# A WKV recurrence on one core: separate pools for k, v and outputs become one set of 19 buffers, and the order of loads and stores changes with it

## The chip, the cores and the metric

The kernel runs on one core of a Trainium2 chip. The metric is the device time of one execution, in microseconds. Four compute engines take part: PE (TensorE, matrix products), DVE (VectorE), ACT (ScalarE) and POOL (GpSimd). SP (SyncE) issues nearly all transfers. Each engine runs its own instructions in order and meets the others only through semaphores.

## The reference

For each of 16 sequences and 256 channels the reference walks along 2048 time steps. It keeps a numerator `aa`, a denominator `bb` and a running maximum `pp`, and puts out a weighted mean of the values so far:

```python
def reference(w, u, k, v):                 # k, v: (16, 2048, 256) float32
    ...
    for t in range(seq_len):
        kk, vv = k[b, t, :], v[b, t, :]
        ww = u + kk
        qq = np.maximum(pp, ww)
        e1, e2 = np.exp(pp - qq), np.exp(ww - qq)
        output[b, t, :] = (e1 * aa + e2 * vv) / (e1 * bb + e2 + 1e-08)
        ww = pp - w + kk
        qq = np.maximum(ww, kk)
        e1, e2 = np.exp(ww - qq), np.exp(kk - qq)
        aa, bb, pp = e1 * aa + e2 * vv, e1 * bb + e2, qq
```

## The kernel before

The kernel doesn't walk along time. It cuts time into 16 stretches `c` of 128 steps, and the 16 sequences into 4 groups of 4. One unit of work `n` (of `NP` = 64) is one stretch of one group: `c, p = divmod(n, 4)`. A unit's k is a tile of 128 partitions (the time steps) by 4 sequences by 256 channels, 512 KB in float32; its v and its output have the same shape and size.

Within a unit, sums along time are matrix products. On PE, `logs(n)` (L191, with the constant rows of L185) adds decay to k. On ACT, `exps(n)` (L204) takes the exponentials into a ring of 12 units, `EZR`. On DVE, `times_v(n)` (L214) multiplies them with v. Then `den` (L341) and `num` (L358) sum denominators and numerators on PE by triangular matrices. The division is done by logarithms: on ACT, `den_log` (L346) writes the logarithm of the denominator into a tile `rd`, and `den_exp` (L349) turns it in place into the reciprocal. On DVE, `mult` (L362), once for each half, multiplies the numerator in, again in place, and `store` (L365) sends the tile out. The state that goes from one stretch to the next is worked out for four units at once by small operations on POOL, DVE and ACT (`state_...`, `copy_sums`, `turn`, `turn_back`), and `inject` puts it into `EZR` by four small transfers, from POOL's queue, for the last stretch from SP's.

The order of the work is written out by hand. Loop turn `n` is called a slot here. Slots 0 to 9 (`LAG` = 10) only fill the ring. From slot 10 to 63, slot `n` takes the exponentials of unit `n` and divides unit `q = n - 10`, with the last products of `qp = n - 11`. A tail then divides the last eleven units. `later` holds the small work of the state by slot and place.

DVE reads k and v once each, and with that the raw tile is done with. `round_k(n + 2)` in slot `n` (L176) copies k of unit n+2 into a rounded tile; `cast_v` (L209) copies v to bf16. The casts are spread unevenly over four slots:

```python
        if n % 4 in (3, 0):
            cast_v(n)
        ...
        elif n % 4 < 2:
            cast_v(n + 1)
```

So a slot with n%4 = 0 has two of them, n%4 = 1 and 3 have one, and n%4 = 2 has none. DVE's order in a slot is: `mult` of the first half, what the state needs, `round_k`, `cast_v`, `mult` of the second half, `times_v`. ACT's order is: `exps`, `den_log`, `den_exp`, with small operations of the state between.

Raw tiles and outputs have pools of their own: `kpool` has 6 buffers, `vpool` 5, `rpool` (for `rd`) 8, 19 tiles of the same size in all. At the head of slot `n`, `load(n + AHEAD)` issues v of unit n+5 and k of unit n+6 (L64, L60), and right behind it `store(qp - 2)` sends out unit n-13. Loads and stores share SP's queue: an issue that waits for a buffer or a result holds up all behind it. At the very end, the output of the last unit goes out in four parts from SP's and ACT's queues (L533), two after each half.

Of the kernel before, what the change touches and what calls it, by code (L numbers as in the profile page):

```python
# [7 lines left out]
F32 = mybir.dt.float32  # L8
# [7 lines left out]
def kernel(  # L16
# [9 lines left out]
    K = tc.keep_in_program_order  # L26
    PE, DVE, SC, POOL, SP = nc.tensor, nc.vector, nc.scalar, nc.gpsimd, nc.sync

    B, T, Dm = k.shape
# [3 lines left out]
    D = 2 * Dm  # L33
    NP = 4 * NST
    RING = 12
    AHEAD = 6
    LAG = 10
    RS = 2.0 ** -20
    CAP = 54.0
    ON_DVE = (0, 1, NST - 1)  # L40

    consts = ctx.enter_context(tc.tile_pool(name="consts", bufs=1))
    kpool = ctx.enter_context(tc.tile_pool(name="kpool", bufs=AHEAD))
    vpool = ctx.enter_context(tc.tile_pool(name="vpool", bufs=5))
    vbpool = ctx.enter_context(tc.tile_pool(name="vbpool", bufs=4))
    rpool = ctx.enter_context(tc.tile_pool(name="rpool", bufs=8))
    small = ctx.enter_context(tc.tile_pool(name="small", bufs=2))
    tiny = ctx.enter_context(tc.tile_pool(name="tiny", bufs=1))
    ps = ctx.enter_context(tc.tile_pool(name="ps", bufs=1, space=bass.MemoryType.PSUM))
# [2 lines left out]
    kr_of, vr_of, VB = {}, {}, {}  # L52

    def rows_of(x, n):
        c, p = divmod(n, 4)
        return x[4 * p:4 * p + 4, c * TC:(c + 1) * TC, :].rearrange("n t d -> t n d")

    def load_k(n, queue=SP):
        kr_of[n] = kpool.tile([128, 4, Dm], F32, tag="kr", name="kr")
        K(queue.dma_start(out=kr_of[n], in_=rows_of(k, n)))  # L60

    def load_v(n, queue=SP):
        vr_of[n] = vpool.tile([128, 4, Dm], F32, tag="vr", name="vr")
        K(queue.dma_start(out=vr_of[n], in_=rows_of(v, n)))  # L64


    def load(n):
        if n - 1 < NP:
            load_v(n - 1)
        if n < NP:  # L70
            load_k(n)

    def matrix(name, dt):
        return consts.tile([128, 128], dt, tag=name, name=name)

    def fill(ap, value):
        K(DVE.memset(ap.bitcast(F32) if ap.dtype == F32R else ap, value))
# [27 lines left out]
    load_k(1)  # L107
    load_row(SP, 1, 2, u)
    load_v(0)
    for n in range(2, AHEAD):  # L110
        load_k(n)
        load_v(n - 1)
    K(SC.preload_act_table_set("natural_log_exp_and_others"))
# [34 lines left out]
    def out_matrices(*names):  # L148
        if "L" in names:
            for h in range(2):  # L150
                fill(Lx[HS * h:HS * h + HS, HS * (1 - h):HS * (2 - h)], 0.0)
        for name in names:
            x, f = I1 if name[0] == "I" else Lx, RS if name[-1] == "N" else 1.0
            mats[name] = matrix(name, BF16)
            K(DVE.tensor_single_scalar(mats[name], x, f, op=ALU.mult))
# [15 lines left out]
    def ez(n):  # L171
        return EZR[:, :, n % RING]

    def round_k(n):
        km = consts.tile([128, 4, Dm], F32R, tag=f"km{n % 2}", name="km") if n < 2 else KM[n - 2]
        K(DVE.tensor_copy(km, kr_of.pop(n)))  # L176
        KM[n] = km

    def logs(n):
        km = KM[n].rearrange("p (i n) d -> p i (n d)", i=2)  # L180

        def rows(q):
            for i in range(2):
                g = 32 * (2 * q + i)
                K(PE.matmul(half(n, q)[:, i, :], CO[g:g + 32, :],  # L185
                            WU[g:g + 32, :].unsqueeze(1).broadcast_to([32, 2, Dm]), start=True, stop=False,
                            tile_position=(g, 0), skip_group_check=True))

        def steps(q):
            for i in range(2):  # L190
                K(PE.matmul(half(n, q)[:, i, :], (NLE, NLZ)[q], km[:, i, :], start=False, stop=True,  # L191
                            skip_group_check=True))

        rows(0)
        rows(1)
        steps(0)
        steps(1)

    def exps(n):
        if n < TURNS:  # L200
            for q in range(2):
                K(SC.activation(ez(n)[:, q], half(n, q), ACT.Exp))  # L202
        else:
            K(SC.activation(ez(n)[:, 0:2], PS[:, 0:4, :].rearrange("p (q i) x -> p q i x", q=2), ACT.Exp))  # L204

    def cast_v(n):
        vb = vbpool.tile([128, 4, Dm], BF16, tag="vb", name="vb")
        vr = vr_of.pop(n)
        K(DVE.tensor_copy(vb, vr))  # L209
        VB[n] = vb  # L210

    def times_v(n):
        vb = VB.pop(n).rearrange("p (i n) d -> p i (n d)", i=2)
        K(DVE.tensor_mul(ez(n)[:, 2:4], ez(n)[:, 0:2], vb.unsqueeze(1).broadcast_to([128, 2, 2, D])))  # L214
# [16 lines left out]
    def sums(n):  # L231
        c, p = divmod(n, 4)
        t = MISC[:, 0:Dm]
        for o in range(2):
            x = 24 - 16 * o - 2 * p
            for j in range(4):
                q, i = divmod(j, 2)
                K(PE.matmul(t[32 * j:32 * j + 32, :], mats["OH"][:, x:x + 32],  # L238
                            ez(n)[:, 2 * q, i, Dm * o:Dm * o + Dm],
                            start=p == 0 and o == 0, stop=p == 3 and o == 1,  # L240
                            tile_position=(0, 32 * j), skip_group_check=True))
# [94 lines left out]
    RD = {}  # L336
# [5 lines left out]
                            skip_group_check=True))  # L342

    def den_log(n, bank=DENB):
        RD[n] = rpool.tile([128, 2, D], F32, tag="rd", name="rd")
        K(SC.activation(RD[n], bank, ACT.Ln, scale=RS))  # L346

    def den_exp(n, i=slice(0, 2)):
        K(SC.activation(RD[n][:, i, :], RD[n][:, i, :], ACT.Exp, scale=-1.0))  # L349
# [10 lines left out]
    def mult(n, bank, i):  # L360
        rd = RD[n]
        K(DVE.tensor_mul(rd[:, i, :], bank, rd[:, i, :]))  # L362

    def store(n):
        K(SP.dma_start(out=rows_of(out, n), in_=RD.pop(n).rearrange("p i (n d) -> p (i n) d", n=2)))  # L365

    later = {}
    for c in range(NST):
# [19 lines left out]
    def small_work(n, where):  # L388
        for f, c in later.pop((n, where), []):
            f(c)  # L390

    def idle_matmuls(n, bank):
        for _ in range(n):
            K(PE.matmul(bank, idle[:, 0:128], idle, start=True, stop=True, skip_group_check=True))
# [5 lines left out]
    K(DVE.scalar_tensor_tensor(WU, WUH, Rest, wuf, ALU.mult, ALU.add))  # L400
    logs(0)
    round_k(1)
    cast_v(0)
    for n in range(LAG):

        load(n + AHEAD)
        exps(n)
        if n % 4 == 0 and n:
            sums(n - 1)
        small_work(n, "act")  # L410
        small_work(n, "logs")
        logs(n + 1)
        if n % 4:
            sums(n - 1)
        small_work(n, "pe")
        idle_matmuls(2, NUMB)
        times_v(n)
        small_work(n, "chain")
        round_k(n + 2)
        small_work(n, "round")  # L420
        cast_v(n + 1)
        if n < 4:
            (state_start, lambda: out_matrices("L"), lambda: out_matrices("IdN", "LN"),
             lambda: out_matrices("Id"))[n]()

    def inverses(n):
        q, qp = n - LAG, n - LAG - 1
        if qp >= 0:
            num(qp, NUMB, 1)

        sums(n - 1)
        if n + 1 < NP:
            recip(q, lambda: small_work(n, "recip"))

    for n in range(LAG, NP):

        q, qp = n - LAG, n - LAG - 1
        load(n + AHEAD)

        if qp >= 2:  # L440
            store(qp - 2)
        if qp >= 0:
            num(qp, NUMB, 0)
        den(q)
        small_work(n, "nums")
        exps(n)
        small_work(n, "act")
        if qp >= 0:
            mult(qp, NUMB, 0)
        small_work(n, "mid")  # L450
        if n == LAG:

            inverses(n)
            small_work(n, "early")
        if n + 2 < NP:
            round_k(n + 2)

        if n % 4 in (3, 0):
            cast_v(n)
        if n + 1 == NP:  # L460
            times_v(n)
        elif n % 4 < 2:
            cast_v(n + 1)
        if n > LAG:
            inverses(n)
        if qp >= 0:
            mult(qp, NUMB, 1)
        small_work(n, "scan")
        if n + 1 < NP:
            times_v(n)  # L470
            small_work(n, "chain")
            logs(n + 1)
        small_work(n, "pe")
# [4 lines left out]
    q, c = NP - LAG - 1, NST - 1  # L478
# [4 lines left out]
    def outputs(n):  # L483
        for i in range(2):
            mult(n, nbank(n, i), i)
        store(n)

    den_log(q)
    den(q + 1, dbank(q + 1))
    sums(NP - 1)  # L490
    copy_sums(c)
    store(q - 2)
    store(q - 1)
    den_exp(q)
    den_log(q + 1, dbank(q + 1))
    tile_num(q, 0)
# [9 lines left out]
    state_offsets(c)  # L506
    state_weights(c)
    mult(q, nbank(q, 1), 1)
    store(q)
    state_chain(c)  # L510
    den(q + 3, dbank(q + 3))
    for i in range(2):
# [14 lines left out]
    n, p = NP - 1, (NP - 1) % 4  # L527
    for i in range(2):
        den_exp(n, slice(i, i + 1))
        mult(n, nbank(n, i), i)  # L530
        for j, eng in ((0, SP), (1, SC)):
            b = 4 * p + 2 * i + j
            K(eng.dma_start(out=out[b, c * TC:(c + 1) * TC, :], in_=RD[n][:, i, Dm * j:Dm * j + Dm]))  # L533
# [31 lines left out]
```

## Time and profile before

| | |
|---|---|
| time, median of 3 runs | 289.74 us (289.18 to 290.79) |
| the profiled execution: time / span | 289.65 us / 288.0 us |
| busy PE / DVE / ACT / POOL | 261.4 / 262.3 / 254.7 / 105.2 us |
| read from HBM / written | 67.12 MB / 33.55 MB |
| mean rate over the span | 353 GB/s |
| issue to landing, k / v / output (median) | 8.3 / 8.3 / 8.1 us |

The span runs from the first to the last event of the core in the trace. The busy time of an engine is the time in which it carried out an instruction; PE's is modelled. The DMA share is the mean over the core's 16 DMA engines and can read over 1, since packets overlap. A row of a timeline has the start, the length, the engine, the line of the kernel, the operation, what it writes and reads, and in brackets the idle time before it with what ended it. A row of the waits has the waiting engine and line, what it waited for, the total in us, the number of times and the longest.

### The profile page before, as it was taken

The numbers are of one execution on the slowest core, as the hardware profiler recorded it, in microseconds if no ns is written. First come the engines' busy times: TensorE is split into PE (matmuls) and PEld (weight loads), VectorE is DVE, ScalarE is ACT, GpSimd is POOL, SyncE is SP. The second block draws the span as 40 slices with busy tenths as digits, with TensorE's granted clock in tenths as the row PEclk, the third lists the DMA queues.
The fourth block names the chain that finished last, engine by engine and source line by source line (L and its number), as shares of the span: only waits on it lengthen the run. The fifth ranks groups of instructions, "written<-read, shape, count | busy, mean of one in ns | idle before, by whom it ended". The sixth has DMA issues, their size and how long they took to land. (4 is left out here: it accounts for less than half of the span.)

```text
span 288.0 us, 5023 instructions
## 1 busy us (share of the span) xinstructions
PE 261.4 (91%) x1694; PEld 119.4 (41%) x1694; DVE 262.3 (91%) x463; ACT 254.7 (88%) x252; POOL 105.2 (37%) x208
## 2 busy tenths in 40 slices
PE   5997897999999999999999999899998989998990
PEld 1443443544444544435444444344344444433430
DVE  4698999999999999999999999998999999988863
ACT  2675678999999999999999989999998999998891
POOL 7000523352534454543525364460434435233000
PEclk9799999999999999999999999999999999999997
DMA  6999999999999999999999999999999999994697
GB/s 214 353 348 350 349 331 349 331 361 375 381 369 381 372 379 378 381 379 381 378 376 381 369 381 375 377 376 371 373 374 380 374 377 380 373 383 160 201 339 245
DMA packets 103587, 101.54 MB, mean 353 GB/s; under 512 B 4285, under 2 KB 103561, under 8 KB 103561
## 3 DMA queue, kind: packets, MB, share of 16 engines
q1 hardware_dynamic: 101336, 100.45, 102.6%
q0 software_dynamic: 1920, 0.50, 0.8%
q8 instruction: 13, 0.21, 0.3%
q10 hardware_dynamic: 304, 0.27, 0.3%
q14 instruction: 14, 0.11, 0.1%
HBM read 67.12 MB, written 33.55 MB: 350 GB/s over the span
## 5 line engine op out<-in xcount | busy, mean ns | idle before, releaser
L204 ACT ACTIVATE EZR<-PS 128x2048 bf16<-128x2048 f32 x54 | 101.2, 1875 | 7.5 <-PE PS L191 6.5
L362 DVE TENSOR_TENSOR rd<-PS,rd 128x512 f32<-128x512 f32 x128 | 87.0, 687 | 6.1 <-ACT rd L349 4.7
L214 DVE TENSOR_TENSOR EZR<-EZR,vb 128x2048 bf16<-128x2048 bf16 x64 | 78.1, 1220 | 2.2 <-ACT EZR L202 1.5
L349 ACT ACTIVATE rd<-rd 128x1024 f32<-128x1024 f32 (+1 forms) x65 | 67.9, 1047 | 2.7 <-DVE rd L362 1.8
L346 ACT ACTIVATE rd<-PS 128x1024 f32<-128x1024 f32 x64 | 65.7, 1026 | 0.8 <-PE PS L341 0.8
L358 PE MATMUL PS<-EZR,LN 128*128 128x512 bf16 x128 | 48.7, 381 | 12.2 <-DVE rd L362 8.4
L331 POOL DMA_DIRECT2D EZR<-cb x60 | 36.5, 614 | 52.1 <-DVE cb L326 45.4
L176 DVE CAST km<-kr 128x1024 fp32r<-128x1024 f32 x64 | 44.7, 699 | 6.9 <-DMA kr<-in_k_dram 6.4
L191 PE MATMUL PS<-km,NLE 128*128 128x512 f32 x128 | 47.5, 453 | 2.3 <-DVE km L176 2.2
L358 PE MATMUL PS<-EZR,IdN 128*128 128x512 bf16 x128 | 48.4, 378 | 0.0
L209 DVE CAST vb<-vr 128x1024 bf16<-128x1024 f32 x64 | 43.4, 694 | 0.7 <-DMA vr<-in_v_dram 0.7
L191 PE MATMUL PS<-km,NLZ 128*128 128x512 f32 x128 | 40.6, 398 | 0.0
L341 PE MATMUL PS<-EZR,Id 128*128 128x512 bf16 x128 | 38.1, 379 | 0.0
L341 PE MATMUL PS<-EZR,L 128*128 128x512 bf16 x128 | 38.1, 379 | 0.0
L185 PE MATMUL PS<-WU,CO 32*128 32x512 bf16 x256 | 27.2, 388 | 3.4 <-DVE WU L400 2.2
L269 POOL TENSOR_TENSOR F<-LL,LL 128x32 f32<-128x32 f32 x13 | 6.7, 515 | 61.9 <-ACT LL L260 61.9
L191 PEld LDWEIGHTS PS<-km,NLZ 128*128 128x128 f32 x128 | 24.4, 191 | 5.8
L191 PEld LDWEIGHTS PS<-km,NLE 128*128 128x128 f32 x128 | 19.3, 190 | 17.3 <-issue 12.9
L238 PE MATMUL PS<-EZR,OH 128*32 128x256 bf16 x512 | 26.1, 278 | 0.1
L202 ACT ACTIVATE EZR<-PS 128x1024 bf16<-128x1024 f32 x20 | 19.4, 1019 | 7.6 <-PE PS L191 7.6
L358 PEld LDWEIGHTS <-IdN 128*128 128x128 bf16 x128 | 12.5, 97 | 28.7 <-issue 26.3
L282 POOL TENSOR_TENSOR Q<-P,F 128x64 f32<-128x64 f32 x13 | 15.7, 1205 | 15.0 <-DVE P L273 15.0
(71 smaller groups left out, 200.0 us busy)
## 6 DMA issues: line engine op xcount, KB each, us to landing
kr<-in_k_dram SPq DMA_DIRECT2D x64, 512.0 KB, 8.3
vr<-in_v_dram SPq DMA_DIRECT2D x64, 512.0 KB, 8.3
out_dram<-rd SPq DMA_DIRECT2D x63, 512.0 KB, 8.1
EZR<-cb POOLq DMA_DIRECT2D x60, 8.0 KB, 5.3
out_dram<-rd SPq DMA_DIRECT2D x2, 128.0 KB, 2.7
out_dram<-rd ACTq DMA_DIRECT2D x2, 128.0 KB, 2.2
EZR<-cb SPq DMA_DIRECT2D x4, 8.0 KB, 1.9
wuf<-in_w_dram ACTq DMA_DIRECT2D x1, 8.0 KB
```

The costliest lines, as they stand in the source:

```text
L176: K(DVE.tensor_copy(km, kr_of.pop(n)))
L185: K(PE.matmul(half(n, q)[:, i, :], CO[g:g + 32, :], WU[g:g + 32, :].unsqueeze(1).broadcast_to([32, 2, Dm]), start=True, stop=False, tile_p ...
L191: K(PE.matmul(half(n, q)[:, i, :], (NLE, NLZ)[q], km[:, i, :], start=False, stop=True, skip_group_check=True))
L204: K(SC.activation(ez(n)[:, 0:2], PS[:, 0:4, :].rearrange("p (q i) x -> p q i x", q=2), ACT.Exp))
L209: K(DVE.tensor_copy(vb, vr))
L214: K(DVE.tensor_mul(ez(n)[:, 2:4], ez(n)[:, 0:2], vb.unsqueeze(1).broadcast_to([128, 2, 2, D])))
L331: K(queue.dma_start(out=EZR[r:r + 1, 2 * q, r0:r0 + 4, :, :].rearrange("o p i (b x) -> o (p i b) x", b=4), in_=cb[x:x + 32, :]))
L341: K(PE.matmul(bank[:, i, :], mats[m], ez(n)[:, q, i, :], start=q == 0, stop=q == 1, skip_group_check=True))
L346: K(SC.activation(RD[n], bank, ACT.Ln, scale=RS))
L349: K(SC.activation(RD[n][:, i, :], RD[n][:, i, :], ACT.Exp, scale=-1.0))
L358: K(PE.matmul(bank, mats[m], ez(n)[:, q, i, :], start=q == 2, stop=q == 3, skip_group_check=True))
L362: K(DVE.tensor_mul(rd[:, i, :], bank, rd[:, i, :]))
```

## The change

The three pools go. `BUFS` = 19 tiles are allocated once, and a list `free` holds each unused one with the slot from which it may be taken. `take(slot)` hands out the tile with the lowest such number, the first in the list where several have it. `round_k` and `cast_v` return their raw tile with the current slot, `store` returns its tile with the slot plus `STORED` = 3. `den_log` takes its tile from the same list.

`loads(n)` now stands behind the casts of slot `n`, and no longer at the slot's head. It loads pairs (v, then k of the next unit) as long as the count is less than nine units ahead of the slot and enough tiles are free, with one kept back for `den_log` from slot 9 on. Stores come behind the loads of the slot. While loads remain, the store in slot `n` is unit n-14 at first, and from slot 24 on one unit later for every six slots; once all loads are issued, everything that is finished goes out. At the very end, both halves of the last reciprocal come ahead of the two products and their transfers.

```diff
-    AHEAD = 6
+    BUFS = 19
+    STORED = 3
...
-    kpool = ctx.enter_context(tc.tile_pool(name="kpool", bufs=AHEAD))
-    vpool = ctx.enter_context(tc.tile_pool(name="vpool", bufs=5))
...
-    rpool = ctx.enter_context(tc.tile_pool(name="rpool", bufs=8))
...
+    free = [(0, consts.tile([128, 4, Dm], F32, tag=f"buf{j}", name="buf")) for j in range(BUFS)]
+
+    def take(slot):
+        j = min(range(len(free)), key=lambda j: free[j][0])
+        assert free[j][0] <= slot
+        return free.pop(j)[1]
+
+    def load_k(n, slot=0):
+        kr_of[n] = take(slot)
+        K(SP.dma_start(out=kr_of[n], in_=rows_of(k, n)))
...
+    loaded = 5
+
+    def loads(slot):
+        nonlocal loaded
+        keep = 1 if slot + 1 >= LAG else 0
+        while loaded < NP and loaded - slot < 9 and sum(x <= slot for x, _ in free) >= 2 + keep:
+            load_v(loaded, slot)
+            loaded += 1
+            if loaded < NP:
+                load_k(loaded, slot)
...
-    def round_k(n):
+    def round_k(n, slot=0):
...
-        K(DVE.tensor_copy(km, kr_of.pop(n)))
+        kr = kr_of.pop(n)
+        K(DVE.tensor_copy(km, kr))
+        free.append((slot, kr))
...
-    def cast_v(n):
+    def cast_v(n, slot=0):
...
+        free.append((slot, vr))
...
     def den_log(n, bank=DENB):
-        RD[n] = rpool.tile([128, 2, D], F32, tag="rd", name="rd")
+        RD[n] = take(n + LAG).rearrange("p (i n) d -> p i (n d)", i=2)
         K(SC.activation(RD[n], bank, ACT.Ln, scale=RS))
...
-    def store(n):
-        K(SP.dma_start(out=rows_of(out, n), in_=RD.pop(n).rearrange("p i (n d) -> p (i n) d", n=2)))
+    def store(n, slot):
+        rd = RD.pop(n).rearrange("p i (n d) -> p (i n) d", n=2)
+        K(SP.dma_start(out=rows_of(out, n), in_=rd))
+        free.append((slot + STORED, rd))
...
-        load(n + AHEAD)
         exps(n)
...
-        round_k(n + 2)
+        round_k(n + 2, n)
         small_work(n, "round")
-        cast_v(n + 1)
+        cast_v(n + 1, n)
+        loads(n)
...
-        load(n + AHEAD)
-
-        if qp >= 2:
-            store(qp - 2)
         if qp >= 0:
             num(qp, NUMB, 0)
...
         elif n % 4 < 2:
-            cast_v(n + 1)
+            cast_v(n + 1, n)
+        loads(n)
+
+        while stored < (qp - 2 - max(0, n - 18) // 6 if loaded < NP else qp):
+            store(stored, n)
+            stored += 1
         if n > LAG:
             inverses(n)
...
     copy_sums(c)
-    store(q - 2)
-    store(q - 1)
+    for n in range(stored, q):
+        store(n, q + LAG)
...
     for i in range(2):
         den_exp(n, slice(i, i + 1))
+    for i in range(2):
         mult(n, nbank(n, i), i)
         for j, eng in ((0, SP), (1, SC)):
```

More of the change, by code (lines that the diff above doesn't have):

```diff
@@ L56, in rows_of, with load_v @@
         return x[4 * p:4 * p + 4, c * TC:(c + 1) * TC, :].rearrange("n t d -> t n d")
[L58 to L71, printed above, removed]
+    free = [(0, consts.tile([128, 4, Dm], F32, tag=f"buf{j}", name="buf")) for j in range(BUFS)]
[6 more added lines that the diff above has]
+        K(SP.dma_start(out=kr_of[n], in_=rows_of(k, n)))
+    def load_v(n, slot=0):
+        vr_of[n] = take(slot)
+        K(SP.dma_start(out=vr_of[n], in_=rows_of(v, n)))
+    loaded = 5
[7 more added lines that the diff above has]
+                load_k(loaded, slot)
     def matrix(name, dt):
@@ L109 @@
     load_v(0)
-    for n in range(2, AHEAD):
+    for n in range(2, 6):
         load_k(n)
@@ L424 @@
              lambda: out_matrices("Id"))[n]()
+    stored = 0
     def inverses(n):
@@ L455 @@
         if n + 2 < NP:
-            round_k(n + 2)
+            round_k(n + 2, n)
         if n % 4 in (3, 0):
-            cast_v(n)
+            cast_v(n, n)
         if n + 1 == NP:
@@ L485, in outputs @@
             mult(n, nbank(n, i), i)
-        store(n)
+        store(n, n + LAG)
     den_log(q)
@@ L508 @@
     mult(q, nbank(q, 1), 1)
-    store(q)
+    store(q, q + LAG)
     state_chain(c)
```

## The prediction

> **What bounds the kernel now.** I read the slices of the page first (DMA share, GB/s), then busy time by stretches, then the waits, and last the timeline of one slot, because only there the order of two engines shows.
>
> ```profile
> DMA  6999999999999999999999999999999999994697
> GB/s 214 353 348 350 349 331 349 331 361 375 381 369 381 372 379 378 381 379 381 378 376 381 369 381 375 377 376 371 373 374 380 374 377 380 373 383 160 201 339 245
> ```
>
> DMA is full from the second slice to 260 us and falls to 160 GB/s while the last outputs are computed. By stretches (us; PE, PEld, DVE, ACT, POOL; clock; DMA share; GB/s):
>
> ```profile
> 120.00:140.00 20.00, 19.58 (x131) 8.86 (x129) 19.70 (x36) 19.81 (x20) 8.90 (x18) 1.00 1.09 380
> ...
> 220.00:240.00 20.00, 18.33 (x124) 8.36 (x124) 18.76 (x30) 18.59 (x20) 8.58 (x17) 1.00 1.08 377
> ...
> 260.00:265.00 5.00, 4.91 (x30) 2.12 (x28) 4.36 (x15) 4.26 (x7) 1.68 (x5) 1.00 0.47 157
> ```
>
> At 120 us DVE and ACT have no gap; at 220 us both lose over a microsecond in 20 at the same DMA rate. Who waits (total, times, longest):
>
> ```profile
> ACT EZR L204 <- PE PS L191: 6.5, 11, 1.4
> DVE km L176 <- DMA kr<-in_k_dram: 6.4, 17, 0.9
> ```
>
> Of those 17 waits for k, 14 lie after 165 us. The starts of `exps(n)` (L204) in the timeline give the slots: slot 15 at 59.70, slot 41 at 162.93, slot 63 at 256.77. So the pitch is 103.23/26 = 3.970 us, then 93.84/22 = 4.265. The DMA queue explains the second: k20 is issued at 59.40 and k63 at 242.07, 43 slots of three transfers, 182.67/129 = 1.416 us each, 4.25 a slot. **Compute needs 3.97 a slot, DMA 4.25; the lead of the loads is used up near slot 41, and from there DMA sets the pace.** Now slot 25 on the two full engines:
>
> ```profile
> 99.36 1.89 ACT L204 ACTIVATE EZR<-PS 128x2048 bf16<-128x2048 f32 x1
> ...
> 100.26 0.68 DVE L362 TENSOR_TENSOR rd<-PS,rd 128x512 f32<-128x512 f32 x1
> ...
> 100.86 0.69 DVE L176 CAST km<-kr 128x1024 fp32r<-128x1024 f32 x1
> ...
> 101.28 1.06 ACT L346 ACTIVATE rd<-PS 128x1024 f32<-128x1024 f32 x1
> ...
> 101.46 0.69 DVE L209 CAST vb<-vr 128x1024 bf16<-128x1024 f32 x1
> ...
> 102.38 1.06 ACT L349 ACTIVATE rd<-rd 128x1024 f32<-128x1024 f32 x1
> ...
> 103.43 1.88 ACT L204 ACTIVATE EZR<-PS 128x2048 bf16<-128x2048 f32 x1
> ...
> 104.04 0.68 DVE L362 TENSOR_TENSOR rd<-PS,rd 128x512 f32<-128x512 f32 x1
> ```
>
> The reader is to see that the logarithm of the denominator (`den_log`, L346) starts at 101.28, while the casts of the same slot (L176, L209) end at 101.55 and 102.15. Today the two have nothing to do with each other.
>
> **What the Trainium skill says.** "DMA: Bandwidth & Descriptors", section "Anatomy of one DMA — SWDGE (gpsimd) path": DMA engines don't wait on semaphores, the issuing sequencer does, before dispatch. The trace agrees: SP's own waits name L64 and L365, the longest 5.1 us, with all later issues behind. "ScalarE: Activation LUTs", "What ACT_TABLE_LOAD costs": back-to-back ACTIVATEs overlap by some 93 ns. Here an `exps` of 1.88 is followed by its successor after 1.77 (103.43, then 105.20): 110 ns. "HBM Reference", "Specifications (TRN2)": a core alone can stream about 425 GB/s. This trace shows no more than 383 in any slice, so I use the measured 1.416 us.
>
> **The change, part by part.**
>
> *Order of the transfers: −6.5 us.* I wrote the rules of `take`, `loads` and the store loop out slot by slot. Ahead of v63 there were 46 stores, now 40. By the end of slot 20, 64 transfers are asked for, by the end of slot 59, 167: 103 in 39 slots, 2.64 × 1.416 = 3.74 us a slot, less than compute's 3.97. Loads start the stretch ahead (six more of them precede the first store), so k is no longer late. 22 slots × (4.265 − 3.970) = 6.5. What is late next is the work on ACT and DVE.
>
> *The shared buffers: a new wait of `den_log`, +11.3 us.* Before, its buffer came from a pool of its own, stored long ago. Now it takes the buffer with the lowest slot number, and loads have taken theirs first. Written out for slots 15 to 60, 26 of 46 get the buffer of a v cast in that same slot, 11 that of the k rounded in it, 9 one whose store is three slots old. ACT must wait until DVE has read it. Behind it in ACT's queue stand `den_exp` and the next `exps`; for these wait DVE's `mult` and `times_v`, and PE's next `logs`.
> The size: ACT could start `den_log` 1.77 after `exps` (2.04 where n%4 is 1, the state's Ln lies between). DVE's first `mult` starts L after `exps`; each further operation follows after 0.60, the last lasts 0.69; n%4 = 3 has a copy of 0.21 between; a hand-over takes 0.04 (DVE at 273.03 after ACT's end at 272.99). A buffer comes free at L + 1.89 after one cast, L + 2.49 after two. L was 0.90 and 0.61 in slots 25 and 26; it can't be under 0.15, as `den_exp` ends 0.11 into `exps`. With L = 0.15 the waits are 0.91 (5 slots with n%4 = 0, second cast), 0.31 (6, first cast), 0.04 (8, n%4 = 1), 0.52 (7, n%4 = 3), none for k: 4.55 + 1.86 + 0.32 + 3.64 = 10.4. With L = 0.6 the same 26 slots give 22.1 and k's 2.3: 24.4. Since a late ACT pulls L to its floor, I take 0.25: 10.4 + 26 × 0.10 = 13.0. Slot 18 takes the buffer of store 1. That is the tenth transfer after k19 (issued at 55.12, done with at 56.5), so issued near 69.3 and landed near 77.4 (8.1 later, the median of 63 stores); `den_log` wants it at 71.65 + 1.77 and the 1.8 that slots 15 to 17 have waited, 75.2: nothing to 3, I take 2. Off goes the air that ACT has: per four slots 4 × (1.77 + 0.96 + 0.95) + 0.30 + 0.27 + 0.27 = 15.56, 3.89 a slot against 3.97, 46 × 0.08 = 3.7. So 13.0 + 2 − 3.7 = 11.3. The ends: 10.4 − 3.7 = 6.7, and 17.3 (L = 0.3, 3 us for the store, no air: 14.3 + 3).
>
> *The end: −1.2 us.*
>
> ```profile
> 282.38 0.36 ACTq L533 DMA_DIRECT2D out_dram<-rd  x1
> 282.80 0.63 ACT L349 ACTIVATE rd<-rd 128x512 f32<-128x512 f32 x1 [1.84 <-DVE rd L362]
> 283.46 0.69 DVE L362 TENSOR_TENSOR rd<-PS,rd 128x512 f32<-128x512 f32 x1 [1.11 <-ACT rd L349]
> ```
>
> The second exponential stood behind ACT's own store issue, which waited for the first product. With both exponentials first, the second product follows the first (start 281.66) at 282.26 in place of 283.46. Its numerator is there (PE ends at 281.80).
>
> *Costing nothing.* In slots 0 to 10 the order of loads is the same and SP issues without a pause from 3 to 55 us, so nine ahead brings none earlier; cover: the full queue. Issuing behind the casts costs no more than the lead: late in the run k(n+5) is issued in slot n and due in slot n+3, 11.9 us for a landing of 8.3; k63, issued in slot 59, has 8 us, so 0 to 1 us if the queue is full. In slot 60 nine stores go out at once and five follow: 14 × 1.54 (0.524 MB at the 340 GB/s of 275 to 280 us) = 21.6 us, done some 10 us into the tail, where `inject` goes on the same SP queue (266.77, 10.0 after slot 63). Its rows are read 6.4 us later and need 4.4, so 2 us cover it: 0, at most +1.5.
>
> Sum: −6.5 + 11.3 − 1.2 = +3.6 on the profiled execution's 289.65 (span 288.0, 1.65 around it; the median of runs, 289.74, is 0.1 higher): **293.2 us**.
>
> **Rivals.** (a) *Faster*: the wait is covered, because DVE gets so far ahead that the cast ends before `den_log` could start. Then −6.5 − 1.2: 282; with half of the wait 287.6. It decides where waits less ACT's air fall under 7.7 us. For it: the 9 buffers from stores and 11 from k give ACT time to come back; against it: the floor of L, since DVE's first product itself waits for ACT. (b) *No change*: all waits at the floor: −6.5 + 6.7 − 1.2 = −1.0, 288.7. (c) *Much slower*: L stays at 0.6, each cast pushes the next: −6.5 + 24.4 − 3.7 − 1.2 = +13, 302.7. Against it: a waiting ACT lets DVE catch up. (d) The change doesn't reach what it says: with buffers short, loads lead by nine pairs only to slot 13 and by five at slot 54. But the 2.64 transfers a slot come from that count, so DMA still has room; should k be late again from slot 41, the wait counts in 26 slots only: 26 × 11.3/46 − 1.2 = +5.2, 294.9.
>
> **The numbers.** My forecast has 0.58, (c) 0.04, (d) 0.05: slower 0.67. Faster, (a): 0.22. Within 0.5%, (b) (1.4 us, about what a measurement of this kernel can tell from no change): 0.11. The range, 284.5 to 297, leaves out the fully covered wait (about 0.12) and the upper tail (0.07).
>
> **What would show it.** Right: L346 waits for DVE's L176 and L209 in the list of waits, over 10 us in all; no wait of km for k after 165 us; a pitch near 4.2 from slot 15 on, even in the stretch that ran at 3.97; DMA below full after 100 us; L349's last wait gone. Wrong: ACT at 19.8 of 20 us and a pitch of 3.97 to slot 63, or k still late.

## The result and the profile after

| | before | after |
|---|---|---|
| time, median | 289.86 us (4 runs) | 303.37 us (4 runs, 302.55 to 304.83) |
| ratio after / before | | 1.0469 [1.0418, 1.0521] |
| profiled execution: time / span | 289.65 / 288.0 us | 302.55 / 300.8 us |
| busy PE / DVE / ACT | 261.4 / 262.3 / 254.7 us | 258.7 / 264.1 / 255.1 us |
| `exps` of slot 15 / of slot 63 start at | 59.70 / 256.77 us | 59.99 / 269.31 us |
| pitch, slots 15 to 41 / 41 to 63 | 3.970 / 4.265 us | 4.469 / 4.233 us |

The change costs 13.5 us. The prediction had 3.6 us, with the right sign and a range that ended at 297 us. The engines do the same work; what grew is the time between slots, and almost only up to slot 41. On the page of the kernel after, the DMA slices (share in tenths, then GB/s) now read:

```profile
DMA  7999999999999999999999799999979999999697
GB/s 231 351 348 350 345 337 337 345 347 360 385 376 374 383 377 355 378 380 316 362 349 322 227 353 356 330 353 347 339 231 365 301 363 333 363 385 349 200 341 258
```

Before, 369 GB/s was the lowest slice between 72 and 259 us. Now the rate falls to 316 and 227 in slices of that stretch: DMA waits for compute. By stretches (us; PE, PEld, DVE, ACT, POOL; clock; DMA share; GB/s):

```profile
120.00:140.00 20.00, 17.41 (x120) 8.01 (x121) 18.51 (x31) 18.46 (x18) 6.82 (x15) 1.00 1.04 358
220.00:240.00 20.00, 18.07 (x123) 8.48 (x125) 18.80 (x31) 17.84 (x18) 8.66 (x17) 1.00 0.94 303
```

At 120 us, where DVE and ACT had no gap, ACT now loses 1.5 us in 20, DVE 1.5, PE 2.6. No engine took the place of DMA as the bound: all three now have gaps. The list of waits of the kernel after (engine and line, what it waited for; total, times, longest):

```profile
DVE buf L376 <- ACT buf L363: 13.3, 26, 0.9
...
ACT buf L360 <- issue: 5.9, 15, 0.8
ACT buf L360 <- PE PS L252: 5.8, 11, 0.9
...
ACT buf L360 <- PE PS L334: 3.7, 4, 1.1
...
ACT buf L360 <- DMA out_dram<-buf: 3.0, 1, 3.0
...
DVE km L188 <- DMA buf<-in_k_dram: 1.4, 3, 1.1
```

The wait for k is down from 6.4 us to 1.4, and the three waits left all lie before 40 us. Longer slots alone would do that too: experiment 2 has the old order of transfers and no late k behind 40 us either. `den_log` (L360) has 20.4 us of idle time before it, but nothing in the list says that it waits for DVE's casts. A line of its own view points to it. Before and after:

```profile
L346 ACTq EVENT_SEMAPHORE  x56: 17/17/38, 71.7 to 276.0; - x56
```

```profile
L360 ACTq EVENT_SEMAPHORE  x64: 17/1929/3511, 38.8 to 289.1; - x64
```

In front of a `den_log` stands a semaphore instruction (min, median, max ns): a wait of ACT's queue ahead of the operation. Before, 56 of the 64 had one, all but as many as `rpool` had buffers, so it seems to stand for the buffer, and it took 17 ns. Now all have one, with a median of 1929 ns. PE's result is the second thing waited for, and the list puts most of the idle time down to PE, or to "issue". So the order must be read in the timeline. Slot 31 (n%4 = 3), one engine beside the other:

```profile
132.62 1.87 ACT L217 ACTIVATE EZR<-PS 128x2048 bf16<-128x2048 f32 x1
132.85 0.44 DVE L318 TENSOR_TENSOR CB<-AB,G 128x128 bf16<-128x128 f32 x1
133.09 0.72 DVE L376 TENSOR_TENSOR buf<-PS,buf 128x512 f32<-128x512 f32 x1
133.78 0.29 DVE L340 CAST cb<-PS 128x128 bf16<-128x128 f32 x1
133.99 0.68 DVE L188 CAST km<-buf 128x1024 fp32r<-128x1024 f32 x1
...
134.59 0.69 DVE L222 CAST vb<-buf 128x1024 bf16<-128x1024 f32 x1
...
135.36 1.03 ACT L360 ACTIVATE buf<-PS 128x1024 f32<-128x1024 f32 x1 [0.88 <-PE PS L334]
...
137.38 1.86 ACT L217 ACTIVATE EZR<-PS 128x2048 bf16<-128x2048 f32 x1
```

`exps` ends at 134.49. `den_log` starts at 135.36, 0.08 after the cast of v (L222) ends at 135.28; the bracket names PE's L334, which has long been done. The next `exps` comes 4.76 after the last. The DVE product (L376) that opens the chain of casts starts 0.47 after `exps`: DVE is still at the state of the slot before (L318 ends at 133.29; its result goes through PE and comes back by the copy L340).

The prediction's L, the time from `exps` to that first product, is thus 0.47 here. (In slots 27, 39 and 51 it is 0.33, but then the copy L340 waits for PE, and the cast of v is done 2.64 after `exps` there and 2.66 here.) In slot 28 (n%4 = 0) it is 0.12:

```profile
120.23 1.86 ACT L217 ACTIVATE EZR<-PS 128x2048 bf16<-128x2048 f32 x1
120.35 0.69 DVE L376 TENSOR_TENSOR buf<-PS,buf 128x512 f32<-128x512 f32 x1 [0.50 <-ACT buf L363]
...
121.56 1.29 DVE L222 CAST vb<-buf 128x1024 bf16<-128x1024 f32 x2
122.33 1.03 ACT L360 ACTIVATE buf<-PS 128x1024 f32<-128x1024 f32 x1 [0.24 <-PE PS L252]
```

(The row with x2 is both casts; `den_log` takes the buffer of the first, done at 122.25.) And slot 18 stands for the output of unit 1, whose store has not landed:

```profile
74.24 1.86 ACT L217 ACTIVATE EZR<-PS 128x2048 bf16<-128x2048 f32 x1
79.09 1.02 ACT L360 ACTIVATE buf<-PS 128x1024 f32<-128x1024 f32 x1 [2.99 <-DMA out_dram<-buf]
...
81.20 1.87 ACT L217 ACTIVATE EZR<-PS 128x2048 bf16<-128x2048 f32 x1
```

Slot 18's pitch, from its `exps` to the next, is 6.96 us. Sorted by what the slot's `den_log` takes, the 48 pitches from slot 15 to 63 fall into few values:

| slot n%4 | what is taken | pitch, us | over the unwaited slot | slots |
|---|---|---|---|---|
| 0 | v, second cast of the slot | 4.85 | 0.97 | 5 |
| 0 | v, first cast | 4.24 | 0.36 | 6 |
| 1 | v | 4.44 | 0.38 | 8 |
| 1 | k | 4.05 | 0 | 3 |
| 2 | k | 4.10 | 0.23 | 3 |
| 3 | v | 4.75 (slot 15: 4.99) | 0.90 | 7 |
| 3 | k | 4.14 (slot 19: 3.85) | 0.28 | 5 |
| 2 | old store (slot 18) | 6.96 | 3.1 | 1 |

Slots without a wait have 3.88, 4.06, 3.87 and 3.85 for n%4 = 0 to 3, a mean of 3.915. Two of these rest on one slot each: 3.88 on slot 60, and 3.85 on slot 19, right behind the stall of slot 18. Over them, the surplus sums to 18.3 for the casts and 3.1 for slot 18.

### The profile page after: what moved, and what is told of

Read it like the earlier page. It is cut to its first block, busy times and chain, and to the rows that moved or that the text cites. A ratio compares the mean times of both kernels' runs of the same rounds, so it can differ in the third digit from the quotient of the medians.

```text
span 300.8 us, 4998 instructions
## 1 busy us (share of the span) xinstructions
PE 258.7 (86%) x1662; PEld 121.5 (40%) x1694; DVE 264.1 (88%) x463; ACT 255.1 (85%) x252; POOL 98.1 (33%) x208
## 4 chain that ended last, share of the span: by engine, by line
ACT 24%; DVE 19%; PE 15%; issue 9%; DMA 3%; DVEq 0%; POOL 0%; ACTq 0%
ACT buf L360 10%; ACT buf L363 8%; DVE buf L376 6%; DVE km L188 6%; ACT EZR L217 6%; PE PS L204 6%; DVE EZR L228 3%; PE PS L355 3%; PE PS L372 2%; PE PS L198 2%; DMA EZR<-cb 2%; DVE vb L222 2%; DMA buf<-in_k_dram 2%; PE PS L269 1%; DVE cb L340 1%
## 5 line engine op out<-in xcount | busy, mean ns | idle before, releaser
L376 DVE TENSOR_TENSOR buf<-PS,buf 128x512 f32<-128x512 f32 x128 | 87.3, 690 | 17.5 <-ACT buf L363 13.3
L360 ACT ACTIVATE buf<-PS 128x1024 f32<-128x1024 f32 x64 | 65.7, 1026 | 20.4 <-issue 5.9
L363 ACT ACTIVATE buf<-buf 128x1024 f32<-128x1024 f32 (+1 forms) x65 | 67.8, 1047 | 0.9
L372 PE MATMUL PS<-EZR,LN 128*128 128x512 bf16 x128 | 48.8, 381 | 12.4 <-DVE buf L376 11.6
L188 DVE CAST km<-buf 128x1024 fp32r<-128x1024 f32 x64 | 45.1, 705 | 1.5 <-DMA buf<-in_k_dram 1.4
L222 DVE CAST vb<-buf 128x1024 bf16<-128x1024 f32 x64 | 43.3, 693 | 0.8 <-DMA buf<-in_v_dram 0.8
L372 PE MATMUL PS<-EZR,IdN 128*128 128x512 bf16 x112 | 42.4, 378 | 0.0
L355 PE MATMUL PS<-EZR,Id 128*128 128x512 bf16 x115 | 35.3, 379 | 0.0
L283 POOL TENSOR_TENSOR F<-LL,LL 128x32 f32<-128x32 f32 x13 | 4.0, 309 | 79.3 <-ACT LL L274 79.3
L204 PEld LDWEIGHTS PS<-km,NLE 128*128 128x128 f32 x128 | 19.2, 190 | 17.5 <-issue 12.9
L372 PEld LDWEIGHTS <-IdN 128*128 128x128 bf16 x128 | 12.5, 98 | 24.9 <-issue 21.9
L252 PEld LDWEIGHTS <-OH 128*32 128x32 bf16 x512 | 9.1, 94 | 31.5 <-issue 31.5
```

Source lines behind the costliest of these rows:

```text
L188: K(DVE.tensor_copy(km, kr))
L355: K(PE.matmul(bank[:, i, :], mats[m], ez(n)[:, q, i, :], start=q == 0, stop=q == 1, skip_group_check=True))
L372: K(PE.matmul(bank, mats[m], ez(n)[:, q, i, :], start=q == 2, stop=q == 3, skip_group_check=True))
```

## Experiments

Each ratio is to the kernel before, timed beside the experiment (medians of 289.56 to 290.20 us).

**1. Take the buffer at the head of the slot.** Only the choice of `den_log`'s buffer moves ahead of this slot's casts, to one that DVE gave back in an earlier slot (`x[2]` is 1 for a stored output, and none is taken). The order of loads and stores stays nearly that of the kernel after: worked out from the two programs, 23 of its pairs of loads come one slot later, none comes earlier, and all stores stay in their slots.

```diff
+        if n + 1 < NP:
+            held[q] = take(n, key=lambda x: (x[2], x[0]))
...
-        RD[n] = take(n + LAG).rearrange(...)
+        tile_ = held.pop(n) if n in held else take(n + LAG)
```

> The changed kernel, but den_log's tile is taken from the list at the head of the slot, and only from tiles that DVE gave back in an earlier slot. Order of loads and stores nearly as in the changed kernel. Theory W (the wait of den_log for this slot's casts is the cause): the pitch falls from 4.36 to the 3.97 that slots 15 to 41 had before, no k is late, slot 63 starts near 250.5, and with the tail of the changed kernel (31.5) the time is 283.7, between 282 and 286.5. Rival O (late stores, loads held back by the free list and SP's waits are the cause): 300 or more, since all of that stays.

Measured: 287.07 us, ratio 0.9918 [0.9893, 0.9943]. The timeline has slot 15 and slot 63 at

```profile
61.36 1.85 ACT L216 ACTIVATE EZR<-PS 128x2048 bf16<-128x2048 f32 x1
...
252.01 1.88 ACT L216 ACTIVATE EZR<-PS 128x2048 bf16<-128x2048 f32 x1
```

190.65/48 = 3.972 us a slot to the end of the loop, in place of 3.970 and then 4.265. In slot 32 (n%4 = 0):

```profile
128.91 1.88 ACT L216 ACTIVATE EZR<-PS 128x2048 bf16<-128x2048 f32 x1
...
130.68 1.02 ACT L360 ACTIVATE buf<-PS 128x1024 f32<-128x1024 f32 x1
130.76 1.29 DVE L221 CAST vb<-buf 128x1024 bf16<-128x1024 f32 x2
...
132.80 1.89 ACT L216 ACTIVATE EZR<-PS 128x2048 bf16<-128x2048 f32 x1
```

`den_log` starts 1.77 after `exps`, before the casts of v have begun. Its semaphore instruction is short again:

```profile
L360 ACTq EVENT_SEMAPHORE  x64: 17/38/38, 38.9 to 272.7; - x64
```

So the one choice of buffer, in a change of several parts, makes the whole slowdown. What the new order of transfers brings, once nothing else holds the slots up, is 197.07 − 190.65 = 6.4 us. The time, 287.07, is above the 283.7 that was expected and above its range, which ended at 286.5: slot 15 comes later here than in the kernel after, by 1.4 us, and the tail from slot 63 takes 33.6 us in place of 31.5 (experiments 7 and 8).

**2. The wait in the old order.** The kernel before, with its loads, stores and end where they were, but 19 shared tiles and a table that gives each `den_log` the same kind of buffer as in the kernel after (the stall of slot 18 excepted).

```diff
+    LAST = {0: 'v8', 1: 'k12', 2: 'k14', ..., 51: 'k62', 52: 'v60'}
...
-        RD[n] = rpool.tile([128, 2, D], F32, tag="rd", name="rd")
+        RD[n] = take(n + LAG, n).rearrange("p (i n) d -> p i (n d)", i=2)
```

> The kernel before with its own order of loads and stores and its own end; only the tiles are shared, and den_log gets by a written table the tile of the same k or v as in the changed kernel (where that one took a store's tile, an old one). W: the waits alone make 18.4 us over slots 15 to 62 by the classes of the changed kernel's trace, slot 63 starts near 266, time near 299; DMA never sets the pace, because 4.30 a slot is over its 4.25. O: no more than the 289.7 of before, within 1.5.

Measured: 300.12 us, ratio 1.0374 [1.0347, 1.0402]; slots 15 and 63 at

```profile
60.09 1.88 ACT L212 ACTIVATE EZR<-PS 128x2048 bf16<-128x2048 f32 x1
...
266.63 1.87 ACT L212 ACTIVATE EZR<-PS 128x2048 bf16<-128x2048 f32 x1
```

206.54 us against 197.07. Slot 63 was expected near 266. The prices by class are those of the table above, within 0.03 us. Slot 41 stands at 173.48, so the pitch is 4.361 up to there and 4.234 behind. Up to slot 41 the wait costs 26 × (4.361 − 3.970) = 10.2 us. Behind it, where DMA set 4.265 before, it costs nothing: the loads are asked for later, and no k is late. The two limits take each other's place, they don't add up. That is also why the kernel after shows nothing of its 6.4 us.

**3. The latest cast in every slot.** The kernel after, but `den_log` takes the tile that DVE gave back last.

```diff
-        RD[n] = take(n + LAG).rearrange(...)
+        RD[n] = take(n + LAG, key=lambda x: (x[2], -x[0], -[y is x for y in free].index(True)) if n + LAG < NP else x[0]).rearrange(...)
```

> The changed kernel, but den_log takes the tile whose reader on DVE comes last in this slot: the second cast where n%4 is 0, the only cast where it is 1 or 3, the rounded k where it is 2; none from a store. W, with the price of each class read off the changed kernel's slots (0.97, 0.38, 0.90, 0.23 over 3.88, 4.06, 3.85, 3.87): waits of 29.5 in place of 18.4, less the 3.1 of slot 18, so 8.0 more: 311.4, pitch 4.53. Rival (sharing as such costs, whichever tile of the slot it is): 300 to 304.

Measured: 311.73 us, ratio 1.0772 [1.0744, 1.0801]; slots 15 and 63 at

```profile
64.97 1.88 ACT L216 ACTIVATE EZR<-PS 128x2048 bf16<-128x2048 f32 x1
...
279.37 1.88 ACT L216 ACTIVATE EZR<-PS 128x2048 bf16<-128x2048 f32 x1
```

214.40/48 = 4.467 us a slot. Within four slots the pitches are 4.74 (n%4 = 3), 4.84, 4.43 and 3.86. The price of a v is that of its class in the kernel after, in all 36 slots, so the wait comes from which cast the buffer had. A k at n%4 = 2 was priced at 0.23 and costs nothing here. In the kernel after, the slots that paid for a k all stand behind a slot without a wait, and L is 0.50 in slot 30; here the slot before has waited, and DVE has caught up. So the price of a k depends on the slot before. It also answers rival (c): each late cast does not push the next, or these pitches would grow.

That the time is so near to the expected 311.4 is chance. From slot 15 to 63 it is 5.1 us more than in the kernel after, not 8.0. Another 5.0 us lie before slot 15, where slots 10 to 14 wait too and TensorE had about half its clock for a while (last section).

**4. Slot 18 alone.** The kernel after, but the `den_log` of slot 18 doesn't take the buffer of the store still on its way.

```diff
+        RD[n] = take(n + LAG, key=lambda x: (x[2] if n == 8 else 0, x[0])).rearrange(...)
```

> The changed kernel, but in slot 18 alone den_log takes no store's tile; it then gets the k rounded in the slot. Theory W: the one stall of ACT on a store's landing (3.0 us) goes and 0.2 comes, all other slots keep their waits to within 0.3: 300.6, slot 18 at 4.1 in place of 6.96. Rival: the stall only moves to another slot that takes a store's tile, since SP is late throughout: 303 to 304.

Measured: 301.31 us, ratio 1.0393 [1.0369, 1.0417]. In the timeline, slots 18 and 19:

```profile
76.01 1.86 ACT L216 ACTIVATE EZR<-PS 128x2048 bf16<-128x2048 f32 x1
...
79.87 1.88 ACT L216 ACTIVATE EZR<-PS 128x2048 bf16<-128x2048 f32 x1
```

The pitch of the slot is 3.86 in place of 6.96 (4.1 was expected, but the k costs nothing behind a slot that has waited); from slot 15 to 63 it is 206.48 us in place of 209.32. So the stall is worth some 2.8 us on the path. The medians differ by 2.1 us, and the spans of the profiled executions by 0.2, since slot 15 comes 1.8 us later in this one (61.77 in place of 59.99) and the tail from slot 63 takes 0.9 us more.

**5. The end alone.** The kernel before, with only the end edit.

```diff
     for i in range(2):
         den_exp(n, slice(i, i + 1))
+    for i in range(2):
         mult(n, nbank(n, i), i)
```

> The kernel before with the last edit alone: both halves of the last reciprocal ahead of the two products. W and the prediction: 1.2 us less, 288.6, last product 1.2 nearer to the last den_log (5.72 to 4.51 from its start to the product's end). Rival: no difference, the end being set by the landing of earlier stores.

Measured: 289.77 us, ratio 1.0008 [0.9996, 1.002]: nothing. The products did move together in its timeline (x4: both of unit 62, both of unit 63, without a gap), and from the last `den_log` to the end of the last product it is 4.51 us in place of 5.72, just the 1.2 that the prediction had. But in its windows behind them:

```profile
284.00:285.00 1.00, 0.00 (x0) 0.00 (x0) 0.02 (x1) 0.00 (x0) 0.00 (x0) 1.00 1.04 350
285.00:286.00 1.00, 0.00 (x0) 0.00 (x0) 0.00 (x0) 0.00 (x0) 0.00 (x0) 1.00 1.03 340
286.00:287.00 1.00, 0.00 (x0) 0.00 (x0) 0.00 (x0) 0.00 (x0) 0.00 (x0) 1.00 0.97 324
```

Hardly an engine works any more, and DMA runs full at 324 to 350 GB/s. The last outputs, 1.05 MB of units 62 and 63, need about 3 us at 340 GB/s, and DMA has no gap before them either; an earlier product then only makes the queue longer. From slot 63 to the end of the span it is 31.2 us before and 31.3 here.

**6. The end with an idle DMA.** To test that reason, both orders of the end again, with the stores of units 60 to 62 left out.

```diff
-        store(n)
+        if n < 60:
+            store(n)
```

> The kernel before without the stores of units 60, 61 and 62 (three of 64 outputs aren't written), to make DMA idle at the end. Theory E (the end is set by the transfers of the last stores, so the end edit alone brought nothing): about 1.0 less than the kernel before, 288.6; this is the base for e9b.

> As e9a_nostores (units 60, 61 and 62 aren't written), with the end edit: both halves of the last reciprocal ahead of the products. Theory E: with DMA idle, the 1.2 us by which the last product comes earlier show: 1.0 to 1.2 less than e9a. Rival: no difference here either, so something other than the last transfers takes the gain.

Measured: 289.48 us, ratio 0.9981 [0.997, 0.9993], with the old end, and 288.12 us, ratio 0.9936 [0.9921, 0.995], with the new one. DMA moves nothing from 281 to 283 us of the first. Leaving the stores out alone brings 0.5 us, where 1.0 was expected. With the transfers out of the way the edit brings 1.4 us (spans 287.9 and 286.5); in the profiled executions 1.1 of it lies behind slot 63. So the step in the prediction was sized right, and hidden behind a resource that the prediction had not looked at there.

**7. Stores less late.** Experiment 1, with the delay of the stores growing more slowly: one unit for every 14 slots, and for every 9, in place of 6.

```diff
-        while stored < (qp - 2 - max(0, n - 18) // 6 if loaded < NP else qp):
+        while stored < (qp - 2 - max(0, n - 18) // 14 if loaded < NP else qp):
```

> The kernel of e1_headtake, but stores are put off one slot further only every 14 slots instead of every 6, so that 5 and not 9 stores go out at once when the loads end, two slots earlier. Theory T (in the tail PE waits for the injected rows, 2.0 us, because their transfer stands behind the burst of stores; what came before is as good as without a wait): pitch stays 3.97, the wait of PE for the injected rows goes, the tail from the start of slot 63 falls from 33.6 to 31.2, and the time from 287.1 to 284.7, to 283.4 if TensorE keeps its full clock near 48 us. Rival D (DMA sets the tail, whatever the order, or stores sent earlier make k late again): 287 to 289, with waits of km for k.

> The kernel of e1_headtake with stores put off one slot further every 9 slots (between its 6 and the 14 of e6_early_stores). If late stores are what keeps k on time (e6 had 4.3 us of waits for k, e1 none), 9 lies between: waits for k of 0 to 2 us, slot 63 near 251.5, tail 32.5, time 286. If the waits for k came from anything else in e6, none here and 285.

Measured: 286.47 us, ratio 0.9872 [0.9848, 0.9896], with 14, and 286.57 us, ratio 0.987 [0.9838, 0.9903], with 9. The list of waits has, with 14 and with 9,

```profile
DVE km L187 <- DMA buf<-in_k_dram: 4.3, 7, 1.6
```

```profile
DVE km L187 <- DMA buf<-in_k_dram: 2.9, 5, 1.1
```

against 1.3 us with 6. Part of this lies near the start in each; behind 60 us it is 2.7 us in 4 waits with 14, 0.5 in one with 9, and nothing with 6. With 14, the pitch stays at 3.97 up to slot 49, and then k is late (slots of 4.93 and 5.72), so that the expected 284.7 was missed. So the late stores are what keeps k in time; the price is a burst at the end. From slot 63 to the end of the span it is 33.6 us with 6, 32.5 with 9 and 32.0 with 14, and 31.2 in the kernel before. The gain and the price nearly balance. These two versions are the fastest of this study, 1.3% below the kernel before; that they are better than experiment 1 is not clear, as its interval reaches down to 0.9893 and theirs up to 0.9896 and 0.9903.

**8. The burst spread out.** Experiment 1, but the stores held back go out two a slot at most, and the last injection but one moves from POOL's queue to SP's.

```diff
+        queue = queue or (SP if c == NST - 2 else POOL)
...
+        most = qp - 2 - max(0, n - 18) // 6 if loaded < NP else min(qp, stored + 2)
+        while stored < most:
```

> The kernel of e1_headtake (stores put off every 6 slots), but once all loads are issued no more than two stores go out in a slot, and the rows of the last but one stretch are injected from SP's queue, ahead of that slot's stores. Theory T (PE's 2.0 us of waiting for these rows come from the burst of nine stores): that wait goes, the tail from slot 63 falls from 33.6 to 31.5, slot 63 stays at 250.5 to 252, time 283.6 to 285.2. Rival: the rows are as late or the stores held back now end later, 286.5 or more.

Measured: 290.42 us, ratio 1.0001 [0.9981, 1.002]: a miss. The wait that it was to remove, in the timelines of the kernel after and of experiment 1:

```profile
277.42 0.59 PE L355 MATMUL PS<-EZR,L 128*128 128x512 bf16 x2 [1.52 <-DMA EZR<-cb]
```

```profile
260.69 0.59 PE L354 MATMUL PS<-EZR,L 128*128 128x512 bf16 x2 [2.01 <-DMA EZR<-cb]
```

It is gone, but in its place the last injection, which goes on SP's queue behind the stores still held back, keeps PE waiting:

```profile
271.55 0.75 PE L355 MATMUL PS<-EZR,L 128*128 128x512 bf16 x2 [4.59 <-DMA EZR<-cb]
```

The moved injection also holds up SP's queue: it waits for its data, the stores behind it wait with it, and DMA stands almost idle for 4 us that it lacks later:

```profile
254.00:258.00 4.00, 3.77 (x30) 1.57 (x30) 3.48 (x6) 3.35 (x6) 0.00 (x0) 1.00 0.14 42
```

Two things were changed at once here, so this run doesn't say how much each is to blame; a spread burst with both injections on another queue was not tried.

## Why the prediction was right or wrong

**What bounded the kernel before: right.** Compute needs 3.97 us a slot, DMA 4.25 behind slot 41. With the order of the transfers changed and no new wait, experiment 1 runs at 3.972 to slot 63.

**Order of the transfers, −6.5: right in size.** Experiment 1 has −6.4. (Ahead of v63 the old order has 45 stores, not 46; the sum doesn't use it.) The sum was right to set the wait against compute's own pace once DMA's is gone. Beside the wait the gain can't be seen: in slots 41 to 63 the wait alone gives 4.234 us a slot and DMA alone 4.265.

**The new wait of `den_log`, +11.3: right mechanism, wrong size.** This is the step that failed. The step is the size of L, taken as 0.25 in all slots. Between the kernel after and experiment 1 lie 209.32 − 190.65 = 18.7 us, 7.4 more than forecast:

- *"Since a late ACT pulls L to its floor, I take 0.25."* Among the slots that take a v it does so only where n%4 = 0: L is 0.12 in slot 28, and the class with the second cast was priced at 0.91 + 0.10 and measured 0.97. Where n%4 = 3, L is 0.33 to 0.47 (0.70 in slot 15), as DVE first finishes the state, and with 0.33 the copy L340 waits for PE, so that the cast of v ends no earlier. Where n%4 = 1 it is 0.43 (slot 17): `exps` at 69.81, the product at 70.24, because PE comes late to the numerators (L372 at 69.56, done at 70.15), behind `turn` (L269), which waited for ACT's copy in the slot before. The floor holds only if ACT is the last thing that DVE's first product waits for. Where n%4 is 1 and 3 it was not.
- The hand-over was taken at 0.04, a value from DVE after ACT. From DVE to ACT it is 0.08 in slots 28 and 31. And where n%4 is 1, `den_log` could start 1.92 after `exps`, not 2.04: the prediction's own rows of slot 25 have 101.28 − 99.36.
- "None for k" was wrong by 0.23 and 0.28 a slot where n%4 is 2 and 3 and the slot before had no wait. The casts together: 18.3 measured, 13.0 forecast. Of the 5.3 between, v at n%4 = 1 makes 1.9, v at n%4 = 3 makes 2.2 and k 1.8; the n%4 = 0 slots came 0.5 cheaper.
- Slot 18: 3.1, forecast "nothing to 3, I take 2". The upper end was right: store 1 was issued at 71.07 and not near 69.3.
- ACT's air: −3.7 forecast from 3.89 a slot. Unwaited slots of the kernel after have 3.915, and experiment 1 has 3.972: 48 × 0.057 = 2.7.

18.3 + 3.1 − 2.7 = 18.7, what the two kernels differ by. That the three add up is no test, since surplus and air are counted from the same unwaited slots; how the total splits is known only as well as these.

**The end, −1.2: right on the engines, nothing in the time.** The step named ACT and DVE but put the transfers behind them at nothing. Experiments 5 and 6 show the cover.

**The burst, "0, at most +1.5": +0.6.** The prediction looked at the last injection, on SP's queue. The one that suffered is the one before, on POOL's: issued at 271.30, its first rows landed near 277.3, and PE waited 1.52 us for them. The last `den_log` is 22.24 us after slot 63, and was 21.66 before.

The sum for the profiled spans: −6.4 + 18.7, + 0.3 for a later slot 15, + 0.3 from slot 63 to the end (31.5 against 31.2) = +12.9, for 300.8 − 288.0 = 12.8.

**The rivals.** The time came out near (c)'s 302.7, but not by its mechanism: L doesn't stay at 0.6 and casts don't push each other (experiment 3). (a) needed cover that isn't there, and (b) a floor in every slot. (d) is refuted by experiment 1: with `den_log` out of it, DMA has room.

**What would show it.** No wait for k after slot 41, DMA below full and L349's last wait gone: as written; the mean pitch is above 3.97 in both stretches, with 4.47 up to slot 41 where "near 4.2" was said. "L346 waits for DVE in the list of waits" was wrong as a test, because the list gives a double wait to one of its two parts, here the one that was not last.

## What to carry to other kernels

When buffers are shared between engines, the choice of buffer decides which engines wait for each other: of several free ones take one that was given back a slot ago, not one that another engine is still to read in this slot. A floor on a wait ("the late engine lets the other catch up") must be worked out for every kind of slot, from what the first instruction of the chain waits for last there. And a saving of the engines at the very end counted here only with the DMA engines idle then.

## What the runs showed of the hardware

The small transfers of this kernel land late when the queues are full, whichever engine issues them. Of the kernel after, with KB each and the median us to landing:

```profile
EZR<-cb POOLq DMA_DIRECT2D x60, 8.0 KB, 5.6
...
EZR<-cb SPq DMA_DIRECT2D x4, 8.0 KB, 2.0
```

The first are issued amid the loads and stores, the second near the end, with DMA at 66 GB/s from 280 to 282 us. In experiment 8, SP's took 1.8 to 1.9 us from 254 us on, when DMA stood almost idle, and up to 5.0 us from 266 us on, behind the stores. The Trainium skill ("DMA: Bandwidth & Descriptors", "Issuing engines are not separate DMA queues") says that transfers from all engines run on the same 16 DMA engines and interleave. These rows agree: POOL's own queue does not protect its 8 KB from SP's burst.

In experiment 1's profiled execution the granted clock of TensorE was half for 3.4 us near the start of the main loop (columns as in the stretches above; the clock is the third number from the end):

```profile
48.00:51.00 3.00, 3.00 (x9) 1.03 (x8) 2.32 (x4) 1.88 (x1) 1.28 (x4) 0.52 1.10 348
```

PE did 9 matmuls there, and 23 at clock 1.00 in the same 3 us of experiment 2. The clock is 0.50 from 47.48 to 50.90 us. Experiments 3, 4 and 8 have such a stretch too: from 46.5 to 51 us their mean clock is 0.62 each, which makes (1 − 0.62) × 4.5 / 0.5 = 3.4 us if the clock is either whole or half. What it costs isn't shown: slot 15 came at 61.36 in place of 59.7 to 60.1, but at 61.13 in experiment 7 (with 9) at full clock. In experiment 1 it comes within 2 us of 1.82 us in which PE stood idle; idle times of 1.84 and 1.85 at the same place in experiments 2 and 5 left the clock at 1.00. The skill ("TensorE: Matmul & The Clock Gate", "Part 1: The HAM clock gate") speaks of an idle window of some 3.4 us that runs freely, so that the number of slow matmuls varies from run to run. The length of the stretch and the variation agree; an idle time of about half that length ahead of a half-speed stretch is what this trace adds. What set it off here stays open.
